# Seven half-size products for each matrix product of an MLP, with operands of the second stage stored by the first

## The chip, the cores and the metric

The kernel runs on one core of a Trainium2 chip. The core has five engines that run side by side, each through its own instructions in order: TensorE (PE in the profile; PEld is its weight load), VectorE (DVE), ScalarE (ACT), GpSimd (POOL) and SyncE (SP), which here only issues DMA transfers. Matmuls read SBUF and add into one of eight PSUM banks (512 float32 a partition each); DVE and ACT read the banks, POOL can't. DMA engines carry data between DRAM and SBUF. The metric is the time of one execution on the device in microseconds; lower is better.

## What is computed

One layer of a decoder on 2048 tokens of width 1024, in float32: four kinds of token mixers, an output projection with gated residual, and an MLP with gated residual. Only the MLP's computation matters here:

```python
D_MODEL = 1024; SEQ = 2048; D_FF = 4 * D_MODEL
...
        y = jnp.concatenate([y_a, y_b, y_c, y_d], axis=-1) @ w_out[l]
        x = x + (gate1[:, None, :] * y).astype(x.dtype)

        h = _modulate(x, norm_ff_gain[l], shift2, scale2)
        y = jnp.square(jax.nn.relu(h @ w_ff1[l])) @ w_ff2[l]
        x = x + (gate2[:, None, :] * y).astype(x.dtype)
```

`h` is 2048 x 1024, `w_ff1` 1024 x 4096, `w_ff2` 4096 x 1024. To keep float32 accuracy every product in the kernel is three matmuls: an operand is split into a high part that PE takes as it is (float32r) and the low remainder, and high x high, high x low and low x high are added in the bank.

## The kernel before

The program is written with a library that places semaphores by itself and orders the instructions of each engine by a plan of its own; priorities are the order of the program, with exceptions marked `high_priority`. All transfers named below are issued by SP, in order.

*Mixing stage* (up to about 1895 us). Two strands are woven: `strand_a` is attention over four chunks of 512 tokens, `strand_b` the projections, the two recurrent mixers and, per chunk, `w_out_dense` (output projection, L1279) and `second_norm` (L1313). `second_norm` makes the MLP's input: four PE transposes to a bank, ACT scales and shifts it, DVE casts the high part and POOL subtracts to get the low part (`modulate`, L551 to L558); both are stored in DRAM as `h2h_d` and `h2l_d`, one 256 KB piece for each chunk and each k-tile of 128 channels.

*Memory.* Two arenas, `AR` (float32r) and `AF_` (float32), are cut into slots by hand: in `AR` the normalised input `hTh`, `hTl` (32 KB a partition), `LS` and `QS` (attention's keys, values and queries), `TS`, `KS` (high and low parts on their way out); in `AF_` `FA` (attention's rows), `FB` (everything else) and `raws` (weights as loaded). `whi` and `wlo` are two buffers each for the split weights. `w_out_dense` takes its input in the `hTh`/`hTl` space or, after attention, in the `LS`/`QS` space (`hts`, L1331).

*MLP* (from about 1895 us). The tokens go in two halves of 1024 (`hf`). For each half, 16 blocks `b` of 256 hidden columns: `load_w` brings and splits 1 MB of `w_ff1` (ACT casts, POOL subtracts, `split_w` L188), `load_w2` 1 MB of `w_ff2`. For each of two chunks `cc`, `ff1` (L1470) runs 2 x 8 k-tiles x 3 matmuls into one of three banks; ACT applies Relu and Square, DVE squares, POOL subtracts, so that the hidden activations stay in SBUF as high and low parts `rh`, `rl`. `ff2` (L1487) of the chunk before then runs 4 token blocks x 2 column halves x 6 matmuls into one of five banks, and DVE adds each bank to the accumulator `acc` in SBUF (L1508). In the last two blocks of a half the gate is applied, the residual added and the output stored (L1511 to L1516). Each matmul loads 128 x 128 weights and streams 512 columns.

## Time and profile before

| | |
|---|---|
| Median of 3 runs | 3331.63 us (3330.45 to 3335.48) |
| The profiled execution | 3335.55 us, span of its instructions 3333.7 us |
| PE busy, share of the span | 94% |
| DVE, ACT, POOL busy | 55%, 42%, 41% |
| Matmuls | 18166, of which 6144 in the six lines of the MLP |
| Transfers | 427.01 MB, mean 128 GB/s |
| Mean granted TensorE clock | 0.954 of full speed |

The page gives the busy time of each engine over the whole span and in 40 slices; a share over the span mixes the two stages, so the stretches are asked for one by one. A busy PE includes the overlap of one matmul with the next: the number of matmuls in a stretch tells more than their durations. "Granted clock" is the clock that TensorE was allowed, 1.00 being 2.4 GHz and 0.50 being 1.2 GHz.

### The profile page before, as it was taken

To read this page: it belongs to the slowest core of one execution; us is meant where nothing else is said; L and a number is where in the kernel's file an instruction comes from. 1 tells how busy PE (TensorE), PEld (TensorE's weight loads), DVE (VectorE), ACT (ScalarE), POOL (GpSimd) and SP (SyncE) were. 2 spreads that over 40 slices of the span, in tenths; PEclk is the share of its full clock that TensorE was granted. 3 is DMA by queue.
4 is the path that set the end of the run, shared out by engine and by line. 5 is a ranking of instruction groups with operands and counts; after the bars stand their busy time and mean duration, and the time that the engine had idled before them with its cause. 6 is when DMAs were issued, how large, how long until landed. Compare 5 with 4: busy or idle time off the path is not lost.

```text
span 3333.7 us, 50269 instructions
## 1 busy us (share of the span) xinstructions
PE 3130.8 (94%) x18166; PEld 2621.7 (79%) x18166; DVE 1842.0 (55%) x4146; ACT 1391.6 (42%) x3004; POOL 1370.4 (41%) x1136
## 2 busy tenths in 40 slices
PE   6999999898888999998897899999999999999999
PEld 4898989687676888887685888888888888888887
DVE  4466577877779686767877323333235423333336
ACT  3666666455455566655555332222211221221111
POOL 4454343243243455454441533333335533333327
PEclk8999999799897999999897899999999999999999
DMA  7876667345334554463435621111113411111112
GB/s 252 268 270 212 220 228 228 121 124 176 98 119 150 169 159 128 155 224 88 129 105 173 229 79 51 51 51 51 39 46 125 171 51 51 51 50 40 43 46 101
DMA packets 342620, 427.01 MB, mean 128 GB/s; under 512 B 33161, under 2 KB 229860, under 8 KB 340308
## 3 DMA queue, kind: packets, MB, share of 16 engines
q1 hardware_dynamic: 337764, 415.42, 38.8%
q10 hardware_dynamic: 4608, 8.39, 0.7%
q8 instruction: 143, 2.34, 0.3%
q14 instruction: 105, 0.86, 0.1%
HBM read 318.72 MB, written 104.99 MB: 127 GB/s over the span
## 4 chain that ended last, share of the span: by engine, by line
PE 46%; DVE 2%; ACT 1%; DMA 1%; issue 0%; POOL 0%; POOLq 0%; SPq 0%; DVEq 0%; ACTq 0%
PE bank L1504 7%; PE bank L1503 7%; PE bank L1502 7%; PE bank L1478 7%; PE bank L1477 7%; PE bank L1479 7%; PE bank L513 1%; DVE AF L873 1%; PE bank L514 1%; PE bank L515 1%; DVE AF L678 0%; ACT AF L687 0%; PE bank L671 0%; PE bank L138 0%; PE bank L740 0%
## 5 line engine op out<-in xcount | busy, mean ns | idle before, releaser
L193 POOL TENSOR_TENSOR wlo<-AF,whi 128x512 fp32r<-128x512 f32 (+2 forms) x432 | 716.0, 1674 | 612.1 <-ACT whi L190 556.3
L1508 DVE TENSOR_TENSOR AF<-bank,AF 128x512 f32<-128x512 f32 x448 | 306.3, 689 | 470.3 <-PE bank L1504 467.6
L513 PE MATMUL bank<-whi,AR 128*128 128x256 f32 (+1 forms) x1664 | 491.2, 296 | 22.0 <-DMA AR<-yh 11.0
L190 ACT ACTIVATE whi<-AF 128x512 fp32r<-128x512 f32 (+2 forms) x432 | 318.3, 756 | 456.4 <-PE bank L1504 256.9
L515 PE MATMUL bank<-whi,AR 128*128 128x256 f32 (+1 forms) x1664 | 481.5, 291 | 1.5 <-DMA AR<-yl 1.5
L514 PE MATMUL bank<-wlo,AR 128*128 128x256 f32 (+1 forms) x1664 | 482.4, 290 | 0.0
L1484 POOL TENSOR_TENSOR AR<-AF,AR 128x512 fp32r<-128x512 f32 x128 | 166.4, 1300 | 615.5 <-DVE AF L1483 482.8
L1478 PE MATMUL bank<-AR,whi 128*128 128x512 f32 x1024 | 404.8, 395 | 0.0
L1477 PE MATMUL bank<-AR,whi 128*128 128x512 f32 x1024 | 402.1, 393 | 1.6 <-DMA AR<-h2h 1.6
L1503 PE MATMUL bank<-wlo,AR 128*128 128x512 f32 x1024 | 403.6, 394 | 0.0
L1504 PE MATMUL bank<-whi,AR 128*128 128x512 f32 x1024 | 403.6, 395 | 0.0
L1502 PE MATMUL bank<-whi,AR 128*128 128x512 f32 x1024 | 403.5, 394 | 0.0
L1479 PE MATMUL bank<-AR,wlo 128*128 128x512 f32 x1024 | 402.5, 393 | 0.0
L687 ACT ACTIVATE AF<-AF,att_m 128x512 f32<-128x512 f32 (+3 forms) x480 | 311.9, 652 | 163.1 <-DVE att_m L684 153.9
L1481 ACT ACTIVATE AF<-bank 128x512 f32<-128x512 f32 x128 | 76.0, 595 | 706.0 <-PE bank L1479 691.6
L513 PEld LDWEIGHTS bank<-whi,AR 128*128 128x128 f32 x1664 | 325.3, 196 | 34.4 <-DMA AR<-yh 12.5
L1483 DVE TENSOR_TENSOR AF<-AF 128x512 f32<-128x512 f32 x128 | 125.6, 982 | 410.1 <-ACT AR L1482 410.1
L515 PEld LDWEIGHTS bank<-whi,AR 128*128 128x128 f32 x1664 | 323.7, 195 | 6.4 <-issue 2.5
L514 PEld LDWEIGHTS bank<-wlo,AR 128*128 128x128 f32 x1664 | 325.4, 196 | 2.8 <-issue 1.0
L678 DVE TENSOR_SCALAR_CACHE_REDUCE AF<-bank 128x512 f32<-128x512 f32 (+3 forms) x480 | 284.9, 604 | 69.8 <-PE bank L671 37.8
L671 PE MATMUL bank<-AR 97*128 97x512 f32 (+10 forms) x640 | 240.5, 431 | 63.4 <-DVE AF L678 60.7
L740 PE MATMUL bank<-AR 128*128 128x256 f32 (+1 forms) x1152 | 234.5, 310 | 11.7 <-DVE AR L730 9.3
(305 smaller groups left out, 5780.1 us busy)
## 6 DMA issues: line engine op xcount, KB each, us to landing
AF<-in_w_ff SPq DMA_DIRECT2D x128, 512.0 KB
AF<-in_w_in SPq DMA_DIRECT2D x144, 256.0 KB
AF<-in_w_in SPq DMA_DIRECT2D x192, 128.0 KB
AF<-in_w_ada SPq DMA_DIRECT2D x80, 256.0 KB
AR<-kD SPq DMA_DIRECT2D x80, 224.0 KB
AF<-in_x SPq DMA_DIRECT2D x64, 256.0 KB
AF<-in_w_out SPq DMA_DIRECT2D x64, 256.0 KB
AR<-kA SPq DMA_DIRECT2D x40, 256.0 KB
```

The source lines that it names most:

```text
L190: nc.scalar.activation(h, r, AF.Copy)
L193: nc.gpsimd.tensor_tensor(l, r, f32(h), ALU.subtract)
L513: nc.tensor.matmul(o[:, :n], hTh[:, k, t], h[:, k, :n], start=(k == 0), stop=False)
L514: nc.tensor.matmul(o[:, :n], hTh[:, k, t], l[:, k, :n], start=False, stop=False)
L515: nc.tensor.matmul(o[:, :n], hTl[:, k, t], h[:, k, :n], start=False, stop=(k == KT - 1))
L687: nc.scalar.activation(FA[e][:, :w], FA[e][:, :w], AF.Exp, scale=-1.0, bias=mx, accum_out=sz[:, p:p + 1] if n > 1 else z)
L1477: nc.tensor.matmul(o, W[0][:, k, js], h2h[k][:, ct], start=(k == 0), stop=False)
L1478: nc.tensor.matmul(o, W[0][:, k, js], h2l[k][:, ct], start=False, stop=False)
L1479: nc.tensor.matmul(o, W[1][:, k, js], h2h[k][:, ct], start=False, stop=(k == KT - 1))
L1502: nc.tensor.matmul(o, rh[:, j, ts_], W[0][:, j, us], start=(j == 0), stop=False)
L1503: nc.tensor.matmul(o, rh[:, j, ts_], W[1][:, j, us], start=False, stop=False)
L1504: nc.tensor.matmul(o, rl[:, j, ts_], W[0][:, j, us], start=False, stop=(j == 1))
```

## The change

Each product of the MLP, `h @ w_ff1` and `relu(...)**2 @ w_ff2`, is computed by Winograd's form of Strassen's method, one level deep. The operands are seen as 2 x 2 blocks; seven products of blocks, of sums of blocks on both sides, give the four blocks of the result.

*First stage.* For each half of the tokens (`ps_`), `h_operands` loads the four pieces of a k-tile in float32 and makes seven operands, each split by ACT and DVE (`split2`). For each of 16 groups of 256 hidden columns, `Weights.ahead` loads 1 MB of `w_ff1` and makes seven weight operands, up to ten ahead. Products run in the order 1, 5, 6, 2, 7, 3, 4, each 4 k-tiles x 3 matmuls. In the middle groups 1, 6, 7 and 4 add into one bank and 5 and 3 into another, 2 has its own; `up_evict` copies or adds out of the bank between products. In the first and last group of each half the k-tile is the outer loop, over seven banks (`up_evict7`). `up_whole` applies Relu and Square on ACT, makes the seven operands of the second stage by sums on DVE and stores them as `r_d`, in runs of 128 float32.

*Second stage.* The products run one after the other over all eight pairs of token blocks, each with its own bank, in the order 1, 6, 7, 4, 5, 3, 2; the contraction is 16 k-tiles in two halves `h`. `w_operand` loads blocks of `w_ff2` and sums and splits them, `r_operand` loads and splits the activations. Banks are copied by ACT after products 1, 6 and 7 while they go on adding, and `dn_out` finishes an output block after 4, 5, 3 and 2.

*Around it.* `second_norm` stores one float32 piece instead of two parts and is finished inside the mixing stage instead of beside the first MLP blocks. The arenas are cut into tiles of their own in a pool `mix`, in the order FA, TS, KS, AL (LS and QS), AH (hTh and hTl), ST, FB, raws; the pools of the MLP are laid over them, tile by tile, and a new tile waits for the old tiles under it. The tiles of the second stage lie over those of the first in the same way. The MLP has no POOL instruction.

The core of the diff:

```diff
@@ second_norm
-                hi, lo = ring(KS), ring(KS)
-                modulate(o, hi, lo, A2[:, k:k + 1], mod[:, SH2 + k:SH2 + k + 1])
-                nc.sync.dma_start(h2h_d[c][k], f32(hi))
-                nc.sync.dma_start(h2l_d[c][k], f32(lo))
+                f = FB.get()
+                nc.scalar.activation(FB[f][:, :512], o, AF.Identity, scale=A2[:, k:k + 1],
+                                     bias=mod[:, SH2 + k:SH2 + k + 1])
+                nc.sync.dma_start(h2_d[c][k], FB[f][:, :512])
+                FB.put(f)
@@ strand_b
-            left.append((rest, st["h"][0] is hTh))
+            for _ in rest:
+                yield
...
+    mix_pool.__exit__(None, None, None)
+    UO = (1, 5, 6, 2, 7, 3, 4)
+    both = ctx.enter_context(tc.tile_pool(name="mlp", bufs=1, reuse_waits="tile"))
+    NTMP, NWA = 12, 2
+    temps = Slots([both.tile([P, 512], F32, name=f"tmp{i}") for i in range(NTMP)])
+    stage = Slots([both.tile([P, 2048], F32, name=f"stage{i}") for i in range(2)])
+    wu = [tuple(t.rearrange("p k n -> p (k n)")[:, u * 512:(u + 1) * 512] for t in w.tiles)
+          for w in (whi, wlo) for u in range(4)]
+    def split2(dst, x):
+        hi, lo = dst
+        nc.scalar.activation(hi, x, AF.Copy)
+        V(lo, x, f32(hi), ALU.subtract)
...
+    for kt in range(4):
+        for i in UO:
+            hc[i, kt] = tuple(up.tile([P, CT], F32R, name=f"hc{i}_{kt}{q}") for q in "hl")
+        if kt == 0:
+            wa = [tuple(up.tile([P, 512], F32R, name=f"wa{i}{q}") for q in "hl") for i in range(NWA)]
+    WS = Slots(wa + wu)
+    def h_operands(ps_, kt):
+        si = stage.get()
+        raw = stage[si].rearrange("p (q t) -> p q t", q=4)
+        for q in range(4):
+            nc.sync.dma_start(raw[:, q], h2_d[2 * ps_ + q % 2][kt + 4 * (q // 2)])
+        b11, b12, b21, b22 = (raw[:, q] for q in range(4))
+        split2(hc[1, kt], b11)
+        i1, t1 = combine(b12, b11, SUB)
+        split2(hc[5, kt], t1)
...
+        stage.put(si)
...
+    def up_mm(o, w, i, kt, first, last):
+        h, l = (t[:, kt * P:(kt + 1) * P] for t in WS[w])
+        xh, xl = hc[i, kt]
+        nc.tensor.matmul(o, h, xh, start=first, stop=False, skip_group_check=True)
+        nc.tensor.matmul(o, h, xl, start=False, stop=False, skip_group_check=True)
+        nc.tensor.matmul(o, l, xh, start=False, stop=last, skip_group_check=True)
...
+    def up_store(t, ps_, g, i):
+        nc.sync.dma_start(r_d[ps_][i][:, :, g, :], temps[t].rearrange("p (b t) -> p b t", t=P))
+    def up_evict(o, st, ps_, g, i):
+        if i == 1:
+            st["11"] = saved(o)
+        elif i == 5:
+            st["22"] = saved(o)
+        elif i == 6:
+            st["21"] = saved(o)
+        elif i == 4:
+            st["12"] = temps.get()
+            up_whole(st, ps_, g, i, o)
+        else:
+            k = {2: "11", 7: "22", 3: "21"}[i]
+            V(temps[st[k]], o, temps[st[k]], ADD)
+            up_whole(st, ps_, g, i)
...
+    wts.ahead()
+    for kt in range(4):
+        h_operands(0, kt)
+    for ps_ in range(2):
+        for g in range(NG):
+            st = {}
+            if g in (0, NG - 1):
+                os_ = {i: ring(allb) for i in UO}
+                for kt in range(4):
+                    for i in UO:
+                        wts.ahead()
+                        up_mm(os_[i], wts.slot[ps_, g, i], i, kt, kt == 0, kt == 3)
+                        if kt == 3:
+                            WS.put(wts.slot[ps_, g, i])
+                            up_evict7(os_, st, ps_, g, i)
+                    if g and not ps_:
+                        h_operands(1, kt)
+            else:
+                oa, oc = ring(allb), ring(allb)
+                for i in UO:
+                    wts.ahead()
+                    o = oa if i in (1, 6, 7, 4) else oc if i in (5, 3) else ring(allb)
+                    for kt in range(4):
+                        up_mm(o, wts.slot[ps_, g, i], i, kt, kt == 0 and i in (1, 5, 2), kt == 3 and i in (4, 3, 2))
+                    WS.put(wts.slot[ps_, g, i])
+                    up_evict(o, st, ps_, g, i)
+    up_pool.__exit__(None, None, None)
...
+    def r_operand(i, p_, kq):
+        w = rd[i, p_, kq] = RS.get()
+        r = raw2.get()
+        nc.sync.dma_start(raw2[r].rearrange("p (k n) -> p k n", n=P), r_d[p_ // TB][i][:, p_ % TB, 4 * kq:4 * kq + 4, :])
+        split2(RS[w], raw2[r])
+        raw2.put(r)
...
+    for i in DO:
+        for h in range(2):
+            for p_ in range(8):
+                o = banks[p_]
+                ahead(1)
+                for u in range(2):
+                    rs = rd[i, p_, 2 * h + u]
+                    rh, rl = RS[rs]
+                    for k in range(4):
+                        kk = KH * h + 4 * u + k
+                        wh, wl = DS[wd[i, kk]]
+                        c = slice(k * P, (k + 1) * P)
+                        nc.tensor.matmul(o, rh[:, c], wh, start=(i in (1, 5, 2) and kk == 0), stop=False, skip_group_check=True)
+                        nc.tensor.matmul(o, rh[:, c], wl, start=False, stop=False, skip_group_check=True)
+                        nc.tensor.matmul(o, rl[:, c], wh, start=False, stop=(kk == NK - 1 and i in (4, 3, 2)), skip_group_check=True)
+                        if p_ == 7:
+                            DS.put(wd[i, kk])
+                    RS.put(rs)
+                    ahead(0)
+                if h == 0:
+                    continue
+                if i in C:
+                    nc.scalar.activation(C[i][p_], o, AF.Copy)
+                else:
+                    dn_out(o, p_, i)
```

## Rows read from the trace of the kernel before

**Rows 1.** The page: the span, and the busy time of PE.

```profile
span 3333.7 us, 50269 instructions
...
PE 3130.8 (94%) x18166; PEld 2621.7 (79%) x18166; DVE 1842.0 (55%) x4146; ACT 1391.6 (42%) x3004; POOL 1370.4 (41%) x1136
```

**Rows 2.** Stretches: length, busy us of PE, PEld, DVE, ACT, POOL; clock, DMA, GB/s.

```profile
1895.00:3329.00 1434.00, 1431.75 (x6193) 1160.54 (x6192) 523.75 (x686) 309.36 (x428) 552.50 (x310) 1.00 0.21 68
...
2000.00:2200.00 200.00, 200.00 (x864) 162.17 (x863) 66.49 (x90) 42.34 (x56) 71.16 (x38) 1.00 0.17 53
...
2600.00:2620.00 20.00, 20.00 (x88) 16.23 (x87) 13.47 (x17) 2.47 (x4) 10.24 (x8) 1.00 0.64 248
```

**Rows 3.** Grouped instructions, 2000 to 3000 us: busy, mean ns | idle before them.

```profile
L1478 PE MATMUL bank<-AR,whi 128*128 128x512 f32 x720 | 284.5, 395 | 0.0
...
L1504 PE MATMUL bank<-whi,AR 128*128 128x512 f32 x717 | 282.9, 395 | 0.0
```

**Rows 4.** Matmuls of one line: ns min/median/max, first and last start.

```profile
L1477 PE MATMUL bank<-AR,whi x1024: 387/393/501, 1895.0 to 3305.3; 128*128 128x512 f32 x171
...
L1504 PE MATMUL bank<-whi,AR x1024: 388/393/476, 1919.6 to 3328.0; 128*128 128x512 f32 x171
```

**Rows 5.** Elementwise work by line, same columns.

```profile
L1508 DVE TENSOR_TENSOR AF<-bank,AF x448: 674/692/693, 1971.2 to 3297.5; 128x512 f32<-128x512 f32 x150
...
L1483 DVE TENSOR_TENSOR AF<-AF x128: 678/693/2512, 1910.7 to 3307.5; 128x512 f32<-128x512 f32 x128
...
L1481 ACT ACTIVATE AF<-bank x128: 577/599/602, 1909.1 to 3306.2; 128x512 f32<-128x512 f32 x128
...
L1482 ACT ACTIVATE AR<-AF x128: 623/634/644, 1910.0 to 3306.8; 128x512 fp32r<-128x512 f32 x128
...
L1484 POOL TENSOR_TENSOR AR<-AF,AR x128: 1284/1293/1738, 1911.5 to 3308.9; 128x512 fp32r<-128x512 f32 x128
```

**Rows 6.** Instructions in order of time at 2104 us: start, duration.

```profile
2104.39 2.41 POOL L193 TENSOR_TENSOR wlo<-AF,whi 128x1024 fp32r<-128x1024 f32 x1 [0.37 <-ACT whi L190]
...
2105.49 1.85 DVE L1483 TENSOR_TENSOR AF<-AF 128x512 f32<-128x512 f32 x1
```

**Rows 7.** First and last start, by line: projection, MLP loads, attention's output.

```profile
L515 PE MATMUL bank<-whi,AR x1664: 274/281/1202, 45.0 to 1894.8; 128*128 128x256 f32 x170, 128*128 128x268 f32 x15
...
L1523 SPq DMA_DIRECT2D AR<-h2h x32: 319/376/668, 1758.1 to 2598.2; - x32
...
L489 DVE TENSOR_TENSOR AR<-AF,AR x24: 668/693/1762, 203.7 to 1835.7; 128x512 fp32r<-128x512 f32 x24
```

**Rows 8.** Chain of waits about the MLP's start: start, duration, what.

```profile
1790.72 2.56 DMA AR<-yh
...
1895.34 5.66 DMA AR<-h2l
1901.01 6.13 DMA AR<-h2h
```

**Rows 9.** Stretches about the MLP's start, columns as in rows 2.

```profile
1840.00:1850.00 10.00, 5.97 (x27) 5.38 (x27) 3.15 (x13) 4.32 (x14) 0.00 (x0) 0.50 0.52 178
1850.00:1860.00 10.00, 10.00 (x81) 9.77 (x81) 5.77 (x11) 5.15 (x8) 6.87 (x7) 0.94 0.36 135
1860.00:1870.00 10.00, 10.00 (x88) 10.00 (x87) 4.77 (x6) 2.74 (x5) 9.29 (x9) 1.00 0.73 250
...
1880.00:1890.00 10.00, 10.00 (x87) 10.00 (x86) 1.70 (x4) 3.86 (x8) 9.08 (x9) 1.00 0.45 148
...
1900.00:1910.00 10.00, 8.34 (x41) 6.10 (x41) 6.02 (x18) 2.80 (x6) 2.06 (x2) 1.00 1.00 355
```

**Rows 10.** DMA in 1400:1500, 2010:2400, 2590:2620: packets, MB, share of 16 engines.

```profile
q1 hardware_dynamic: 20912, 22.19, 68.4%
...
q1 hardware_dynamic: 11556, 18.30, 15.2%
...
DMA packets 4813, 8.45 MB, mean 282 GB/s; under 512 B 448, under 2 KB 1460, under 8 KB 4811
```

More of the change, by code (lines that the diff above doesn't have):

```diff
@@ L1361, in hybrid_block @@
         ada_blocks = iter(range(8, 24))
-        left = []
         def strand_b():
@@ new lines, in hybrid_block, with saved @@
+    wts = Weights()
+    def up_mm(o, w, i, kt, first, last):
[4 more added lines that the diff above has]
+        nc.tensor.matmul(o, l, xh, start=False, stop=last, skip_group_check=True)
+    def saved(o):
+        t = temps.get()
+        nc.scalar.activation(temps[t], o, AF.Copy)
+        return t
```

332 lines of the change are left out of this document (214 added, 118 removed).

## The prediction

> **What bounds the kernel now.** I read the busy table of the page first, then the tenths over the span, then cuts of the span into stretches. The page has TensorE (PE) at 94% of 3333.7 us [rows 1], but that is a mean of two different stages. From the first MLP matmul to the last there are 1434 us, PE is busy for 1431.75 of them, and the granted clock is 1.00 (2.4 GHz) throughout; VectorE (DVE) is busy for 37%, ScalarE (ACT) for 22% and GpSimd (POOL) for 39% [rows 2]. In the grouped instructions of the middle 1000 us the idle column of the matmul lines is 0.0 [rows 3]. So in the MLP nothing but PE sets the time, and a matmul taken away is worth its spacing there. That is not the 395 ns of the duration column, which overlaps with the next one: 864 matmuls start in 200 us [rows 2], 0.2315 us each. The spacing doesn't move where transfers are dense: 88 in 20 us at a DMA share of 0.64 [rows 2].
>
> **What is taken away.** Six matmul lines (the first and the last in [rows 4]) of 1024 each are 6144. After the change the first stage has 2 halves x 16 groups x 7 products x 4 k-tiles x 3 passes = 2688 and the second 7 x 8 x 16 x 3 = 2688, all of the same shape (128 columns of weights, 512 streamed). That is 5376, 768 fewer, and 768 x 0.2315 = 177.8 us. The sum starts at the profiled execution's 3335.55 us and ends at it less 177.8 if PE streams as before; the rest is what keeps it from streaming.
>
> **What is added on DVE and ACT.** A middle group of the first stage (12 of its matmuls per product, 84 in all) lasts 84 x 0.2315 = 19.4 us on PE. DVE has in it 7 subtractions for the low parts of the weights, 4 sums of weight quarters, 3 additions out of a bank and 4 sums for the second stage's operands, 18. One costs 0.69 us, from a bank or from SBUF [rows 5]: 12.5 us. ACT has 7 high parts, 3 copies and 8 Relu/Square, 18 at 0.60 to 0.63 us [rows 5], 11.2 us. Both lie beside PE. I take the median; the longest DVE square took 2.51, and the one of 1.85 us that I looked at lay under a POOL subtraction of 2.41 us [rows 6]. No POOL instruction is left in the new MLP. Even at 1.0 us each the 18 would stay under the 19.4. In the second stage a step of one bank (24 matmuls) is 5.6 us; DVE has 2 low parts of activations, 1 to 3 operations for a weight and up to 3 for the output, at most 6 x 0.69 = 4.2 us.
>
> **Hand-overs of a bank.** A middle group keeps one bank for products 1, 6, 7, 4 and one for 5, 3. PE must wait until ACT has copied product 1 before 6, product 6 before 7, and until DVE has added product 7 before 4. Behind the waiting matmul stands all of PE's queue. The cover is one product, 12 x 0.2315 = 2.8 us, and the copy or addition needs 0.6 to 0.7. It runs out when three other operations stand ahead on that engine. I take 0.2 us a group, 28 groups, **+6 us**; bounds 0 and 2 us a group (56 us), the upper one being three operations ahead twice in a group.
>
> **Start of the first stage.** Here the change loses most. Now the first MLP matmul starts at 1895.0, 0.2 us after the last one of the output projection [rows 4, 7], because half of its operands were loaded from 1758 on, as ready high and low parts [rows 7]. After the change the operands must be made. Their memory is that of the mixing stage, laid over it in order: the scratch and staging tiles over FA, free when attention ends at about 1836 [rows 7], but the k-tile-0 operands and two weight buffers mostly over KS and AL. AL holds the last projection's input (its other half, AH, was free at 1758, so the loads went there [rows 7]) until 1894.8, and the eight weight buffers cut from whi and wlo are free only then too. From 1895: seven weight operands (DVE 4.9 us, some sums earlier), which release the only staging tile that `h_operands` can have, +6; then four rounds of a 256 KB load, 2.6 us [rows 8], and 11 DVE operations, 7.6 us, one after the other since they share that tile, 4 x 11 = +44; then the last matmuls, +1. That is 51 us for a group with 19.4 us of PE work, and an estimated 5 us for the 49 matmuls beside the MLP's 6144 [rows 2], so **+26 us**. Bounds: +14 if the loads hide behind DVE (55 operations x 0.69 = 38), +40 if a load takes the 5.7 to 6.1 us that the present ones take at the same place [rows 8] and the last norm's own DVE work falls in between. I take the shorter load, since what runs beside it then is one load and not sixteen.
>
> On the clock: from 1840 to 1850, with PE idle for 4 of 10 us, its granted clock was 0.50 (1.2 GHz), and 0.94 in the next 10 us at full work [rows 9]; a dip of PE to 8.3 of 10 us at 1900 left it at 1.00 [rows 9]. The Trainium skill ("TensorE: Matmul & The Clock Gate", section "HAM oscillation — how this bites in real kernels") says that a kernel which waits for operands between its k-tiles falls back to half clock at each of them. The traces so far bear both out.
>
> **Between the halves.** The last group of the first half and the first of the second run k-tile outermost on seven banks. The operands of k-tile 0 may be overwritten 21 matmuls = 4.9 us into the last group; four rounds of 10.5 us end at 47, with the 11 evictions of that group (7.6 us of DVE) partly between them, at most 54. PE wants k-tile 3 at 19.4 + 14.6 = 34. So 13 to 20, **+16 us**; the lower bound is 2, if loads hide (44 x 0.69 + 4.9 = 35).
>
> **From first to second stage.** The weights' buffers lie over k-tile 0 and are made under the last 14.6 us of PE. The activations' buffers come free one by one in the last round and need ACT and DVE, 1.3 us, but the 7.6 us of evictions are in the same DVE queue. Bounds 1.3 and 10, **+6 us**.
>
> **Ahead of the MLP.** The second norm drops 32 casts on DVE and 32 subtractions on POOL (1.3 us each in the MLP [rows 5]) and half of its stores, all beside other work; the mixing stage's tiles are cut anew, which lets the planner order the work differently. I count 0, with bounds of -10 and +15. The last matmul starts at 3328.0 and the span ends at 3333.7 [rows 1, 4], 5.7 us later; the new end is one bank's three DVE operations and a store, the same. The 2 us that PE idles in the MLP now [rows 2] go.
>
> **Sum.** 3335.55 - 177.8 + 6 + 26 + 16 + 6 - 2 = 3209.8 for an execution like the profiled one. The median of the runs shown, 3331.63, lies 3.9 lower: **3206 us**.
>
> **DMA.** Each group of the first stage stores 7 x 256 KB in runs of 512 B and loads 1 MB in runs of 1 KB: 7 x 512 + 1024 = 4608 packets in 19.4 us. Packets averaging 1.06 KB took 68.4% x 16 x 100 us / 20912 = 52 ns in one stretch; in the MLP, averaging 1.6 KB, 15.2% x 16 x 390 us / 11556 = 82 ns [rows 10]. At 52 ns a group's transfers need 4608 x 52 / 16 = 15.0 us, so they hide; most of the new packets are smaller than either mean, so 52 is the nearer row. In the second stage a step moves at most 1.5 MB in 5.6 us, 270 GB/s; 8.45 MB went in 30 us (282 GB/s) at the busiest stretch of the MLP without PE losing a matmul [rows 2, 10]. The Trainium skill ("DMA: Bandwidth & Descriptors", section "Specifications") puts the smallest transfer for line rate at 512 B, just the size of these runs; no store of that size was singled out here.
>
> **The rivals.**
> 1. *Bank hand-overs stall every middle group.* For: DVE and ACT run 12.5 and 11.2 of 19.4 us in strict order, and three different chains share them. Against: the cover is four times one operation. At the 2 us bound, 28 x 2 = 56 instead of 6: 3256. Chance 0.17.
> 2. *The stores bind the first stage*, the case on the other side. If a packet costs the 82 ns of the MLP's own stretch, a group needs 4608 x 82 / 16 = 23.6 us, 4.2 more than PE, x 32 = 134, nearly all of the gain left: 3206 + 134 = 3340. It decides from 81 ns on (a loss of 126 us). For: the number is a row; small runs, written to memory, have no row of their own. Against: bytes, not packets, seem to carry the cost, since the stretch with the larger packets has the higher price. Chance 0.08.
> 3. *The transitions hide.* If the planner makes operands early and loads run ahead, the terms of 26, 16 and 6 shrink to their lower bounds, 14, 2 and 1: 3175. For: DVE is busy for 4.8 of the 10 us from 1860 and 1.7 of those from 1880 [rows 9]. Against: the memory is not free. Chance 0.10.
> 4. *The clock falls between the k-tiles*, at the start and between the halves. A round's 21 matmuls then take 9.7 instead of 4.9 us, still under the 10.5 of DVE and load, except in the last round of each: +5, and +5 while the second group speeds up: 3216. Chance 0.12. It is the Trainium skill's rule named above that would bring this about.
> 5. *The new cut of the tiles lengthens the mixing stage* by 15 us or more, or its end frees memory later: 3225 to 3240. Chance 0.07.
> That the work isn't reduced is excluded by the loops counted above.
>
> **How the numbers follow.** Forecast 0.46, rivals 0.17, 0.08, 0.10, 0.12, 0.07. The range is 3160 (all lower bounds, -10 ahead of the MLP) to 3280: it leaves out rival 2, the worst third of rival 1 and little below. A measurement of this kernel tells 0.2% (7 us) from no change. Faster 0.92, within 0.2% 0.02, slower 0.06; the last two are rival 2.
>
> **What would show it.** Right: 5376 matmuls of 512 in the MLP, 0.23 us apart within groups; PE idle at three places, with DVE or a load named as releaser; POOL at zero there; DVE at 0.69 us. Wrong: PE waits spread evenly over the groups, put down to ACT copies or DVE additions (rival 1), or a DMA share near 0.9 in the first stage with stores behind (rival 2); a first MLP matmul well before or after 1900 to 1910; a spacing other than 0.2315.

## The result and the profile after

The changed kernel takes 3226.77 us (median; its runs go from 3212.16 to 3231.48), the kernel before, measured beside it, 3333.35: a ratio of 0.967, 95% interval 0.964 to 0.971. That is 106.6 us less where 126 were forecast, inside the range of 3160 to 3280. The profiled execution took 3222.74 us, its span 3221.0.

The page of the changed kernel, busy us of the span (before: [rows 1]):

```profile
span 3221.0 us, 50522 instructions
...
PE 2973.0 (92%) x17398; PEld 2494.0 (77%) x17398; DVE 2053.9 (64%) x4642; ACT 1650.5 (51%) x3576; POOL 777.6 (24%) x800
```

Stretches of it, columns as in [rows 2]: a stretch of middle groups of the first stage, the change from the first stage to the second, and the only part of the second stage where PE waits:

```profile
2000.00:2240.00 240.00, 240.00 (x1043) 196.66 (x1042) 152.66 (x238) 135.30 (x231) 0.00 (x0) 1.00 0.52 154
...
2560.00:2620.00 60.00, 52.04 (x207) 41.70 (x206) 33.20 (x58) 26.21 (x47) 0.00 (x0) 0.89 0.69 221
...
2900.00:3000.00 100.00, 94.91 (x398) 73.66 (x397) 52.63 (x84) 28.83 (x52) 0.00 (x0) 1.00 0.68 217
```

In the middle groups PE is busy for all of the 240 us at a clock of 1.00, as before. VectorE is now at 0.64 there (0.33 in the 200 us of [rows 2]), GpSimd has nothing left, and the DMA share is 0.52. The MLP lasted 1433.2 us, from the last output-projection matmul (1894.8, [rows 7]) to the last matmul (3328.0, [rows 4]); now it lasts 1312.7, to 3215.6. The projection's last matmul itself comes 8.1 us later. One line of it, columns as in [rows 4]:

```profile
L523 PE MATMUL bank<-whi,AL x128: 275/280/582, 1837.9 to 1902.9; 128*128 128x256 f32 x128
```

From here on *lost* time is the length of a stretch less its MLP matmuls times their spacing, which is 0.2303 us within the first stage (19.35 us for a group of 84) and 0.2313 in the second. The places in order, for all kernels that ran; "later" is the rest of the second stage. Each row is one profiled execution, and a figure is good to some 0.3 us:

| kernel | last projection matmul | start | middle of a half | between halves | change of stage | later | span |
|---|---|---|---|---|---|---|---|
| changed kernel | 1902.9 | 36.7 | 0.0 | 9.7 | 16.1 | 9.5 | 3221.0 |
| e1_h2_pool | 1922.6 | 28.6 | 0.0 | 10.9 | 15.8 | 11.4 | 3235.5 |
| e1b_h2_last | 1909.5 | 28.5 | 0.0 | 11.7 | 15.7 | 13.0 | 3224.6 |
| e3_gate | 1907.0 | 35.9 | 0.3 | 9.7 | 17.7 | 10.2 | 3228.5 |
| e10_scratch | 1904.0 | 35.6 | 0.0 | 9.9 | 4.9 | 9.1 | 3211.5 |
| e4_dn_pool | 1904.6 | 36.0 | 0.0 | 10.1 | 15.8 | 11.1 | 3228.0 |
| e11_lag | 1900.8 | 35.7 | 0.0 | 9.7 | 15.8 | -0.4 | 3207.7 |
| e5_all | 1908.7 | 28.5 | 0.0 | 10.8 | 20.1 | 10.0 | 3233.1 |
| e12_rows | 1873.1 | 36.4 | 0.3 | 7.4 | 15.1 | 8.4 | 3187.1 |
| e13_all | 1866.5 | 27.4 | 0.3 | 6.7 | 5.0 | -0.5 | 3153.5 |
| e9_nosum | 1907.0 | 30.4 | 0.0 | 0.0 | 11.9 | 4.2 | 3199.7 |

The first row adds up: 5376 matmuls are 2688 x 0.2303 + 2688 x 0.2313 = 1240.8 us, and 72.0 lost make 1312.8. Where the gate's rows were moved, the last group of the first stage loses another 2 us, which no column shows.

### The profile page after: what moved, and what is told of

It reads as the page before. It is cut to its first block, busy times and chain, and to the rows that moved or that the text cites. A ratio compares the mean times of both kernels' runs of the same rounds, so it can differ in the third digit from the quotient of the medians.

```text
span 3221.0 us, 50522 instructions
## 1 busy us (share of the span) xinstructions
PE 2973.0 (92%) x17398; PEld 2494.0 (77%) x17398; DVE 2053.9 (64%) x4642; ACT 1650.5 (51%) x3576; POOL 777.6 (24%) x800
## 4 chain that ended last, share of the span: by engine, by line
PE 53%; DVE 13%; DMA 6%; ACT 3%; issue 2%; POOL 1%; SPq 0%; DVEq 0%; POOLq 0%; ACTq 0%
PE bank L1560 6%; PE bank L1561 6%; PE bank L1559 5%; PE bank L1782 5%; PE bank L1781 5%; PE bank L1780 5%; PE bank L142 3%; PE bank L521 2%; PE bank L748 2%; PE bank L523 2%; PE bank L522 2%; PE bank L679 2%; PE bank L734 2%; DMA stage<-in_w_ff 2%; DVE FA L881 2%
## 5 line engine op out<-in xcount | busy, mean ns | idle before, releaser
L197 POOL TENSOR_TENSOR wlo<-raw,whi 128x512 fp32r<-128x512 f32 (+1 forms) x304 | 408.7, 1364 | 387.1 <-ACT whi L194 346.0
L521 PE MATMUL bank<-whi,AH 128*128 128x256 f32 (+1 forms) x1536 | 452.3, 295 | 25.1 <-ACT whi L194 11.1
L522 PE MATMUL bank<-wlo,AH 128*128 128x256 f32 (+1 forms) x1536 | 445.7, 290 | 0.9 <-POOL wlo L197 0.9
L523 PE MATMUL bank<-whi,AH 128*128 128x256 f32 (+1 forms) x1536 | 444.8, 290 | 0.0
L695 ACT ACTIVATE FA<-FA,att_m 128x512 f32<-128x512 f32 (+3 forms) x480 | 310.5, 650 | 153.4 <-DVE att_m L692 146.2
L686 DVE TENSOR_SCALAR_CACHE_REDUCE FA<-bank 128x512 f32<-128x512 f32 (+3 forms) x480 | 284.3, 603 | 69.6 <-PE bank L679 40.0
L521 PEld LDWEIGHTS bank<-whi,AH 128*128 128x128 f32 x1536 | 299.1, 195 | 35.9 <-ACT whi L194 11.4
L522 PEld LDWEIGHTS bank<-wlo,AH 128*128 128x128 f32 x1536 | 299.4, 195 | 3.8 <-POOL wlo L197 1.4
L523 PEld LDWEIGHTS bank<-whi,AH 128*128 128x128 f32 x1536 | 298.4, 195 | 2.7 <-issue 1.9
L679 PE MATMUL bank<-AL 97*128 97x512 f32 (+10 forms) x640 | 241.9, 436 | 57.1 <-DVE FA L686 53.8
L748 PE MATMUL bank<-TS,AL 128*128 128x256 f32 (+1 forms) x1152 | 238.4, 314 | 15.7 <-DVE TS L738 7.2
L734 PEld LDWEIGHTS bank<-ident,FA 128*128 128x128 f32 x1088 | 139.7, 150 | 38.5 <-DVE FA L881 28.5
L509 PE MATMUL bank<-AH,whi 128*128 128x512 f32 x384 | 159.1, 419 | 7.1 <-DVE FB L1107 2.1
L510 PE MATMUL bank<-AH,whi 128*128 128x512 f32 x384 | 159.0, 414 | 2.5 <-DMA AH<-hl 2.5
```

Source lines behind the costliest of these rows:

```text
L197: nc.gpsimd.tensor_tensor(l, r, f32(h), ALU.subtract)
L521: nc.tensor.matmul(o[:, :n], hTh[:, k, t], h[:, k, :n], start=(k == 0), stop=False)
L522: nc.tensor.matmul(o[:, :n], hTh[:, k, t], l[:, k, :n], start=False, stop=False)
L523: nc.tensor.matmul(o[:, :n], hTl[:, k, t], h[:, k, :n], start=False, stop=(k == KT - 1))
L679: nc.tensor.matmul(o[:, :w], lh, rh(p)[:, :w], start=(i == 0), stop=(i == len(mm) - 1 and not diag))
L686: nc.vector.tensor_scalar(FA[e][:, :w], o[:, :w], -1.0, 3.0e38, ALU.mult, ALU.min, accum_out=st[:, p:p + 1])
```

## The experiments

All are edits of the changed kernel, except b_rows, which edits the kernel before. Moving an issue to another queue moves the waits that it stands in, and leaves the bytes and the arithmetic as they were.

### The start of the first stage: e1_h2_pool, e1b_h2_last, e9_nosum

The chain of waits in the changed kernel (start, duration, what), and SyncE's issues in order of time:

```profile
1917.00 6.78 DMA stage<-in_w_ff
1923.80 1.29 DVE tmp L1472 x2
```

```profile
1910.97 0.99 SPq L1330 DMA_DIRECT2D h<-FB  x2
...
1912.98 3.97 SPq L1330 DMA_DIRECT2D h<-FB  x5
1917.00 1.20 SPq L1529 DMA_DIRECT2D stage<-in_w_ff  x2
```

The first load of w_ff1 (L1529) is issued 14.1 us after the last projection matmul, straight behind the last second-norm store (L1330), and lands 6.78 us later. VectorE has nothing from 1910 until that load has landed at 1923.8; then it is the bound:

```profile
1920.00:1930.00 10.00, 0.31 (x1) 0.31 (x2) 6.20 (x11) 4.74 (x9) 0.00 (x0) 0.50 0.68 233
1930.00:1940.00 10.00, 8.84 (x26) 6.17 (x25) 10.00 (x17) 5.73 (x11) 0.00 (x0) 0.66 0.39 127
1940.00:1950.00 10.00, 9.18 (x35) 5.88 (x34) 10.00 (x18) 6.32 (x12) 0.00 (x0) 1.00 0.55 172
1950.00:1960.00 10.00, 9.02 (x37) 6.47 (x36) 10.00 (x18) 5.35 (x10) 0.00 (x0) 1.00 0.20 64
```

```diff
-                nc.sync.dma_start(h2_d[c][k], FB[f][:, :512])
+                nc.gpsimd.dma_start(h2_d[c][k], FB[f][:, :512])        # e1_h2_pool
+                (nc.gpsimd if c == NC - 1 else nc.sync).dma_start(...)  # e1b_h2_last
```

> The stores of the second normalisation's result are issued by GpSimd and no longer by SyncE; nothing else changes. Theory, the queue: in the changed kernel the first load of first-layer weights was issued at 1917.0, on SyncE right behind the last of these stores, 14 us after the last output-projection matmul (1902.9). With the stores on another queue SyncE reaches that load once the output projection's own transfers are issued, at about 1905, so the load lands about 12 us earlier, VectorE begins on the operands at about 1912 in place of 1923.8, and the first MLP matmul comes 9 to 12 us after the last output-projection matmul or a little more (26.8 us before): a gain of 8 to 11 us up to the first steady group. Rival, VectorE sets the start: it has the second normalisation until about 1910 and then the sums of the weights, so an earlier load gains 0 to 2 us.

Measured: the start loses 28.6 us in place of 36.7, the gain of 8 that the queue predicted. The span is longer all the same, since the mixing ended at 1922.6; more on that below. e5_all has the same stores on GpSimd and its mixing ended at 1908.7, so what the move costs ahead of the MLP can't be read from one execution. The next kernel leaves the other chunks alone:

> Only the last chunk's stores of the second normalisation are issued by GpSimd; the other chunks' stay on SyncE. Theory, SyncE's queue: the start of the first stage loses about 8 us less than the 36 us of the changed kernel, as when all chunks' stores were moved (28.5 us in both executions), and the mixing ends as in the changed kernel, 1903 to 1907, so that the gain is seen in the span: 8 us. Rival, the loss at the start follows the end of the mixing and not the queue: 34 us or more.

Measured: 28.5. The load now follows the projection by 2 us:

```profile
1911.47 1.19 SPq L1529 DMA_DIRECT2D stage<-in_w_ff  x2
```

The queue is shown as the cause of 8 us. The span was 3224.6, no better than the changed kernel's: its mixing ended 6.6 us later with PE's order unchanged, and 2.0 and 3.5 us more were lost between the halves and late in the second stage, so the gain is read at the place and not in the total.

```diff
-        i1, t1 = combine(b12, b11, SUB)
-        split2(hc[5, kt], t1)
-        i2, t2 = combine(b22, t1, SUB)
-        split2(hc[6, kt], t2)
+        split2(hc[5, kt], b12)
+        split2(hc[6, kt], b22)
...
```

> The changed kernel without the four sums that make the activations' operands (7 in place of 11 VectorE operations a k-tile): the operands that need a sum take a quarter as it is, so the result is another one; transfers, matmuls and splits are as they were. Theory, VectorE sets the start once the loads are there (10.00 of 10 us busy from 1930 to 1950): four k-tiles of four sums at 0.60 us are 9.6 us, and the loss between the last output-projection matmul and 2000 falls from 36 to 27 us, that between the halves (9.7 us) by 2 to 6. Rival, the staging tile and its loads set it: within 3 us of 36.

Measured: 30.4 at the start, a gain of 6.3, and 9.7 to 0.0 between the halves, more than the 2 to 6 expected. VectorE was still busy for 28.52 us of 1930 to 1960, but PE streamed through the halves' change:

```profile
2250.00:2270.00 20.00, 20.00 (x88) 16.38 (x87) 19.06 (x33) 14.47 (x28) 0.00 (x0) 1.00 0.77 237
2270.00:2290.00 20.00, 20.00 (x88) 16.42 (x87) 19.09 (x32) 15.08 (x28) 0.00 (x0) 1.00 0.66 203
```

So VectorE's operations on operands set the pace of the ramp after the first load, and without the four sums the halves' change costs nothing. In the changed kernel VectorE isn't the last link there, though: 5.9 of the 9.7 us are lost where PE waits for splits of weights behind a weight load that left late (see "Between the halves" below). That the change of stage and the second stage, whose code is the same, lost less as well (11.9 and 4.2) was not expected; the order on the queues differs from there on, and I have no run that tells why.

### The change of stage: e3_gate, e10_scratch

The chain of waits in the changed kernel:

```profile
2574.60 5.11 DMA tmp<-r
...
2579.78 5.99 DMA r<-tmp
...
2585.87 0.30 DVE tmp L1742
...
2586.30 2.05 PE bank L1743 x8
```

An operand load (r), the last operand store, VectorE's gate rows (L1742) in a scratch tile that this store gives back, and the gate's small matmuls, behind which the products stand. Moving them ahead of the last group:

```diff
             st = {}
+            if ps_ and g == NG - 1:
+                gt = [gate_bank(u) for u in range(2)]   # in a ring bank and two of the later scratch tiles
...
-    gate2 = [gate_bank(u) for u in range(2)]
+    gate2 = [temps[t] for t in gt]
```

> The two rows of the second gate are spread over the partitions ahead of the last group of the first stage, and no longer at the start of the second. Theory, the gate's place in the queues: TensorE lost 15.5 us between the stages (2569 to 2600), since the gate's eight small matmuls stand in its queue among the first products and wait for scratch that the last operand store gives back (5.4 us twice). Moved ahead, the loss between the stages falls to about 8 us, which is the fall of operand store, load and first product, and the last group of the first stage loses at most 2 us more: gain 6 to 8 us. Rival, the operands' way through memory sets it: the first product of the second stage waits for the stored operands whatever the gate does, and the loss stays within 2 us of 15.5.

Measured: 17.7 us. The gate's place was not what set it. PE's longest wait there, and the chain:

```profile
PE bank L1783 <- ACT wlo L1465: 10.6, 1, 10.6
```

```profile
2580.56 5.18 DMA r<-tmp
...
2585.76 4.85 DMA tmp<-in_w_ff
...
2590.63 0.64 ACT wd3h L1465
```

ScalarE stood at the split of a weight (wd3h) whose load (tmp<-in_w_ff) had to wait for the same last store (r<-tmp) to leave its scratch tile; the split of the operand that PE wanted was behind it in ScalarE's queue. So the next kernel keeps the five scratch tiles out of the ring at first:

```diff
+    held = [raw2.free_.pop() for _ in range(5)]
...
+                if i == DO[0] and h == 0 and p_ == 3:
+                    raw2.put(*held)
                 ahead(1)
```

> The second gate's rows are made ahead of the last group of the first stage, as in the run that moved them alone, and the first weight and operand loads of the second stage use only the eight quarters of the staging tiles; the five scratch tiles of the first stage join them from the fourth group of products on. Theory, the scratch tiles: a weight load that reuses one waits until the last group's result has been stored from it (the store was issued at 2580.6 and took 5.2 us, the load 4.9 us), and ScalarE, which works in order, holds the operands' split behind that weight's: TensorE waited 10.6 us at 2582.6. With the scratch tiles held back the loss between the stages (17.7 us with the gate moved, 16.1 us in the changed kernel) falls to 8 us or less. Rival, the transfers at the change (0.65 to 0.7 of the DMA engines busy there) set it: 12 us or more, since fewer tiles mean fewer loads under way.

Measured: 4.9 us, and fewer tiles under way did no harm (the DMA share even rose, to 0.77):

```profile
2560.00:2620.00 60.00, 57.57 (x240) 46.07 (x239) 36.14 (x57) 27.79 (x49) 0.00 (x0) 0.97 0.77 261
```

Either cure alone leaves the other wait on the same store; I ran the gate's alone, not the scratch tiles' alone.

### The second stage: e4_dn_pool, e11_lag

```diff
-        nc.sync.dma_start(temps[ti], x1_d[t][:, us])
+        nc.gpsimd.dma_start(temps[ti], x1_d[t][:, us])
...
-        nc.sync.dma_start(out[0, t * P:(t + 1) * P, us], x)
+        nc.gpsimd.dma_start(out[0, t * P:(t + 1) * P, us], x)
```

> In the second stage the loads of the residual and the stores of the result are issued by GpSimd and no longer by SyncE. Theory, the order on SyncE: the loads of second-layer weights stand there behind a residual load that waits for a scratch tile whose store was issued just ahead of it, so the weights of the next product came late, and TensorE lost 8.5 us at 2930 to 3000 and 1.4 us at about 2705. With the two kinds of transfer on another queue that loss is gone: gain 7 to 10 us. Rival, the load's own traffic or VectorE's sums set it: the loss stays at 7 us or more. The start of the MLP and the change of stage are the changed kernel's own here, so that they also show how far these vary from one execution to the next.

Measured: 9.4 us lost at 2900 to 3010 where the changed kernel loses 8.5: the order on SyncE was not the cause, my theory fell. And the end came later: 9.5 us from the last matmul to the end of the span in place of 5.4, with the last store on GpSimd. What VectorE waited for in the changed kernel at 2900 to 3000 (us in total, times, longest):

```profile
DVE stage L1702 <- DMA stage<-in_w_ff: 24.5, 9, 3.6
DVE tmp L1702 <- DMA tmp<-in_w_ff: 11.7, 4, 3.6
```

13 waits, 36 us: before each subtraction for a weight of the fifth product VectorE stands for a load just issued, and the low part of an operand that PE needs now is queued behind. The cure is to issue the load a step earlier:

```diff
-                w_operand(*wtodo.pop(0))
+                if not loaded:
+                    loaded.append(w_load(*wtodo.pop(0)))
+                if wtodo[1:]:
+                    loaded.append(w_load(*wtodo.pop(0)))
+                w_operand(*loaded.pop(0))
```

> In the second stage the loads of each weight operand are issued one step (5.5 us) ahead of the subtraction and split that read them. Theory, order on VectorE and ScalarE: in the fourth product's second half the fifth product's weights are loaded, two blocks each, and VectorE stands up to 4.2 us before each subtraction (14 waits, 40 us in 2900 to 3000) with the split of an operand that TensorE needs now behind it: TensorE loses 0.5 to 1.3 us a group, 8.5 us in all. With the loads a step earlier the loss of 2900 to 3010 falls to 2 us or less, and that at about 2718 (1.1 us) too. Rival, the 13 scratch tiles and the transfers (0.68 busy, 217 GB/s) set the pace, so an earlier load only waits longer for its tile: 6 us or more.

Measured: nothing is lost any more, though more bytes move in that stretch (238 GB/s, 217 before the edit):

```profile
2900.00:3000.00 100.00, 100.00 (x435) 81.91 (x433) 60.50 (x95) 33.95 (x60) 0.00 (x0) 1.00 0.76 238
```

The span of 3207.7 is 13.3 below the changed kernel's: 9.9 of it here, 2.1 from a mixing that ended earlier.

### The first three moves together: e5_all

> The three moves together: the second normalisation's stores and the second stage's residual loads and result stores go by GpSimd, and the gate's rows are made ahead of the last group of the first stage. Theory, order on the queues is what the changed kernel loses: the gains add up to 21 to 29 us, so 3194 to 3206 us where the changed kernel has a median of 3226.8 and a profiled run of 3222.7. Rival, the three places are limited by transfers and VectorE: 3219 to 3227 us.

Measured: 3234.28 us (3233.07 to 3238.02), slower than the changed kernel. The start's 8 us were gained, the change of stage lost 4 more, the tail was 12.4 us in place of 5.4, and the mixing ended 5.8 later. The tail, the change of stage and the 2 us in the last group of the first stage, some 13 us, are the price of having taken two causes from the names of the waits alone; why the mixing ended later isn't shown.

### Ahead of the MLP: e12_rows, b_rows

Matching VectorE instructions run 16 to 21 us later than in the kernel before from 190 to 1500 us. Some 12 us of it are there by 120 us. Stretches of the kernel before, then of the changed one:

```profile
60.00:80.00 20.00, 19.85 (x155) 19.63 (x154) 5.48 (x14) 6.74 (x17) 7.14 (x8) 0.94 0.74 254
80.00:100.00 20.00, 19.39 (x146) 18.55 (x147) 8.91 (x20) 11.21 (x25) 13.00 (x11) 1.00 0.97 316
```

```profile
60.00:80.00 20.00, 11.01 (x87) 10.03 (x85) 3.03 (x9) 3.88 (x11) 2.48 (x5) 0.83 0.48 159
80.00:100.00 20.00, 14.62 (x96) 14.09 (x97) 3.14 (x12) 7.71 (x15) 10.30 (x9) 0.75 0.91 301
```

PE's weight port waits there for the input projection's weights, once and long:

```profile
PEld bank L521 <- ACT whi L194: 11.4, 1, 11.4
```

SyncE's loads of w_in stop after six and go on 41 us later, behind 48 small stores of constant rows (L454 to L471), 24 of them from the lines that the diff touched (L468, L471):

```profile
36.02 2.95 SPq L208 DMA_DIRECT2D raw<-in_w_in  x6
...
71.16 0.58 SPq L468 DMA_DIRECT2D qB<-FA  x1
71.78 1.15 SPq L471 DMA_DIRECT2D qD<-FA  x2
...
80.25 2.96 SPq L208 DMA_DIRECT2D raw<-in_w_in  x6
```

In the kernel before twelve loads had gone ahead of its rows, from 36.3 to 41.8.

```diff
-                nc.sync.dma_start(qB_d[c][u][P:P + 4, :]...
+                nc.gpsimd.dma_start(qB_d[c][u][P:P + 4, :]...
...
-                    nc.sync.dma_start(qD_d[c][u][384 + 2 * h:386 + 2 * h, :]...
+                    nc.gpsimd.dma_start(qD_d[c][u][384 + 2 * h:386 + 2 * h, :]...
```

> The constant rows of the attention operands (24 small stores, 0.58 us of SyncE each) are issued by GpSimd in place of SyncE. Theory, the recut's rows: in the changed kernel TensorE has no product from 69.1 to 84.5, since the loads of the input projection's weights stop at 38.5 on SyncE and go on at 80.3, behind these rows, where in the kernel before six more loads had gone ahead of them (to 41.8); matching VectorE instructions ran 16 to 21 us later than before from about 190 to 1500, of which 8 us were left at the end of the mixing. With the rows on another queue the hole of 15 us goes, and the last output-projection matmul comes 8 to 17 us earlier than the changed kernel's own (1902.9 to 1907 in three executions): 1888 to 1897, total 3210 to 3219. Rival, the attention's own chain sets the end of the mixing: the hole goes, but the 15 us are waited for later and the end stays within 4 us of 1905.

Measured: 3189.87 us (3184.58 to 3203.52), 0.957 of the kernel before, interval 0.954 to 0.960, and 36.9 below the changed kernel. Twelve loads go ahead again, and PE is busy in the hole:

```profile
37.00 7.02 SPq L208 DMA_DIRECT2D raw<-in_w_in  x12
```

```profile
60.00:80.00 20.00, 15.96 (x130) 15.52 (x129) 3.68 (x14) 6.56 (x17) 17.61 (x22) 1.00 0.75 255
80.00:100.00 20.00, 20.00 (x154) 19.87 (x155) 8.13 (x18) 8.43 (x20) 8.08 (x8) 0.91 0.98 313
```

```profile
L523 PE MATMUL bank<-whi,AL x128: 275/280/583, 1808.6 to 1873.1; 128*128 128x256 f32 x128
```

The projection ended 29.8 us earlier, more than the 8 to 17 expected, and 21.7 before the kernel before's own: against that kernel matching VectorE instructions were 6 us late at 200, even at 1130, 6 early at 1500 and 20 early at 1600. So the hole is shown, and its undoing is worth the larger part of the 15 us by 200 (10 us) and all of it by 600; what else made the rest is open. Is it the rows in themselves? The kernel before with its rows moved:

```diff
-                nc.sync.dma_start(qB_d[c][u][P:P + 4, :]..., negr)
+                nc.gpsimd.dma_start(qB_d[c][u][P:P + 4, :]..., negr)
-                nc.sync.dma_start(qD_d[c][u][384:388, :]...
+                nc.gpsimd.dma_start(qD_d[c][u][384:388, :]...
```

> The kernel before, with nothing changed but that its 16 constant-row stores (8 for each of two operands) are issued by GpSimd. It tells what of the 30 us that the move gave the changed kernel's mixing is the undoing of a loss and what is a gain of its own. Theory, the changed kernel's hole alone: the kernel before has no such hole (its six further weight loads go ahead of the rows), so it stays within 4 us of its 3336 us, and the recut tiles themselves make the mixing some 20 us shorter (last output-projection matmul at 1873.1 with them, 1894.8 before). Rival, the rows stand in the way in both: the kernel before gains 10 to 22 us too, and its last output-projection matmul comes at 1873 to 1885.

Measured: neither. 3360.99 us, 1.008 of the kernel before (1.006 to 1.010), the projection's end at 1919.6, and a hole of its own: no product of the projection starts from 47.0 to 63.5, and PE is idle from 47.2 to 57.2. VectorE and GpSimd there, in order of time:

```profile
45.66 9.35 DVE L344 COPY AF<-AF 32x128 f32<-32x128 f32 x2
48.28 6.73 DVE L374 TENSOR_TENSOR AF<-AF 1x64 f32<-1x64 f32 x1
```

```profile
42.40 4.37 POOL L462 DMA_DIRECT2D qB<-AF  x8 [1.20 <-DVE AF L456]
46.79 1.33 POOL L193 TENSOR_TENSOR wlo<-AF,whi 128x536 fp32r<-128x536 f32 x1
...
52.30 2.57 POOL L193 TENSOR_TENSOR wlo<-AF,whi 128x536 fp32r<-128x536 f32 x2
```

GpSimd issued the rows from 42.4 to 46.8, and the work it had put off ran without a break to 54.9. Until then VectorE stood in the second of two small copies and in a 1x64 product, 9.27 us and 6.73 (they overlap and end together at 55.0; the first copy took 0.20); in the kernel before the two copies took 1.55 and the product 1.32. PE's next matmul needed what VectorE makes behind them. Matching VectorE instructions were 14 us later than in the kernel before at 210 and 25 only from 1800 on, so the hole is at most some 14 of the 25; the rest is open. So the move of the rows is worth what the order around it makes of it, +25 us in one kernel and -30 in the other, and it doesn't isolate what the new cut of the tiles does by itself.

### How far the other engines are: e7_twopass

```diff
     nc.tensor.matmul(o, h, xh, start=first, stop=False, skip_group_check=True)
-    nc.tensor.matmul(o, h, xl, start=False, stop=False, skip_group_check=True)
     nc.tensor.matmul(o, l, xh, start=False, stop=last, skip_group_check=True)
```

> The first stage without the product of the weights' high part with the activations' low part: 1792 matmuls in place of 2688 there, 56 in place of 84 a group, so the result is less exact; all other work is left. It shows how far the other engines are from setting the pace. A group takes 19.35 us now, with VectorE busy 0.64 of it (12.3 us), ScalarE 0.56 (10.9 us) and 154 GB/s. Theory, bank hand-overs and VectorE are hidden also at this pace: a group takes 56 x 0.2303 = 12.9 us and the first stage 206 us less, about 433 us in place of 638.6. Rival, hand-overs or VectorE come next at once: 14 us or more a group, 465 us or more, and the clock may fall in the waits.

Measured: the middle groups of the first half take 12.95 to 13.3 us, those of the second half mostly 14.0 to 14.4 (a few 13 to 15.6), and the first stage 486.3 us. In the first half the hand-overs are hidden even at two thirds of the time, to 0.1 us a group in the mean; in the second ScalarE waits for scratch tiles that are being stored (r<-tmp, 18.4 us in 2250 to 2405). Two of its stretches:

```profile
1960.00:2130.00 170.00, 165.08 (x701) 133.21 (x702) 148.00 (x239) 128.90 (x238) 0.00 (x0) 0.99 0.76 220
2250.00:2400.00 150.00, 141.45 (x592) 110.82 (x591) 117.71 (x187) 102.08 (x188) 0.00 (x0) 1.00 0.71 207
```

The total is above both figures (433 and 465): the first three groups cost 12 us more over their pace than in the changed kernel, the halves' change 23, and the second half's groups some 16.

### The four that helped: e13_all

The edits of e1b_h2_last, e10_scratch, e11_lag and e12_rows in one kernel.

> The four moves that helped, together: the constant rows by GpSimd, the last chunk's second-normalisation stores by GpSimd, the gate's rows ahead of the last group with the scratch tiles held back, and the second stage's weight loads one step ahead. Theory, four places with nothing in common: the gains add up, 8 + 12 + 9 us on the 3189.9 us of the kernel with the rows moved: 3156 to 3168 us. Rival, part of each is waited for again elsewhere (the start of the first stage waits for VectorE, the halves' change for loads): 3170 to 3185 us.

Measured: 3158.31 us (3155.22 to 3160.55), 0.9465 of the kernel before, interval 0.945 to 0.948, 68.5 us below the changed kernel. The gains add up: 27.4 at the start, 5.0 at the change of stage, nothing later. The mixing, too, ended 6.6 us earlier than in e12_rows, with the same order of PE's work, so part of the total is spread.

## Why the prediction was right, and where it was not

The total is right because the main step is, and because errors of 6 to 10 us at seven places partly cancel, which is luck. Against the sum for the profiled execution (3209.8; measured 3222.7), term by term in us:

| step | foreseen | measured | difference |
|---|---|---|---|
| 5376 matmuls streamed | 1248.4 (1433.2 - 177.8, less 2 and 5 named in the text) | 1240.8 | -7.6 |
| hand-overs | 6 | 0.0 | -6 |
| start, with 5 us of other matmuls | 31 | 36.7 | +5.7 |
| between the halves | 16 | 9.7 | -6.3 |
| change of stage | 6 | 16.1 | +10.1 |
| second stage | 0 | 9.5 | +9.5 |
| ahead of the MLP | 0 | 8.1 | +8.1 |

They add to 13.5, against the 12.9 that are missing.

**Matmuls taken away.** Right, and PE streams in both stages. The spacing of 0.2315 was read low: the 864 matmuls of the 200 us count those that reach over the stretch's edges. By the sum's own 1433.2 us less 7, one of the 6144 matmuls took 0.2321 us before. It is now 0.2303 and 0.2313, which over 5376 matmuls makes about 7 of the -7.6; why it fell isn't shown.

**Hand-overs, rival 1.** The cover of one product was the right argument, the 0.2 us a group an allowance for nothing. VectorE's 0.69 us for an operation held (whi<-stage: median 684 ns over 111), and from the fourth group of a half on none lost time. Ahead of that PE did wait for a bank's copy (L1559 behind ACT L1565), in the third group of the first half and the second of the second, 1.3 us in two waits. e7_twopass shows that the cover holds at 12.95 us a group.

**Start.** The size is nearly right by luck, the reason is not. I had the first weights made from 1895 on and a load in series with VectorE in each round (2.6 + 7.6 = 10.2 us, which I took as 11: 3 us too much in four rounds). But the mixing's pool ends as one, and every MLP instruction stands behind every mixing instruction on its queue: the first load left at 1917.0 behind the last second-norm store. So the first MLP matmul came at 1929.7, well after the 1900 to 1910 that the prediction had named, and by its own sign this part of it was wrong. What saved the size is that, once the first load had landed, loads hid behind VectorE (10.00 of 10 us), whose operations started 0.60 us apart and not 0.69, so the ramp was shorter than four rounds. "Each queue that it is moved past" was the question I didn't put to SyncE. e1b_h2_last and e9_nosum show both parts.

**Between the halves.** Too dear by 6.3, and neither the value's rounds nor the lower bound's "loads hide" is what happened. The first group of the second half lost 3.2 us. The group behind it, which the prediction left out, lost 5.9: PE waited there for splits of weights on ScalarE (wlo, L1465), and ScalarE for a weight load that left SyncE only at 2274.51 and took 8.0 us. Ahead of that load stood VectorE's last sum of operands (done at 2273.3) and, on the same queue, stores; which of the two held it isn't shown. The load, and PE's matmuls behind it:

```profile
2274.51 8.00 DMA stage<-in_w_ff
...
2284.78 0.70 PE bank L1559
2285.49 0.43 PE bank L1560
...
2289.17 0.23 PE bank L1561
```

Without the four sums the same load left at 2263.39, and nothing was lost (e9_nosum).

**Change of stage.** I had looked at the buffers of the activations and at VectorE's queue. What set it is a third resource, the scratch tiles from which the last operands are still being stored: weight loads and gate rows wait for them, and ScalarE's order passes the wait on. The upper bound of 10 was too low by 6.

**Second stage.** "No loss" was wrong. I had counted VectorE's time in a step (at most 4.2 of 5.6 us) and not that it works in order: an instruction that waits for a load holds those behind it however idle the engine is (0.53 busy).

**Ahead of the MLP, rival 5.** The bounds of -10 and +15 held, the value of 0 did not. The mechanism is rival 5's only in name: with the same tiles twelve loads of w_in go ahead once the rows are moved (e12_rows), so it was the order on SyncE, in which the planner put six of them behind the rows. Why it did is open.

**DMA, rival 2.** It fell. In the first stage's second half (packets, MB, share of 16 engines):

```profile
q1 hardware_dynamic: 29656, 17.92, 60.0%
```

0.600 x 16 x 100 / 29656 us = 32 ns a packet at a mean of 0.6 KB, less than the 52 and far from the 81 from which it would have decided. The Trainium skill ("DMA: Bandwidth & Descriptors", section "Specifications") wants transfers of 512 B for line rate; with runs of just that size the trace agrees so far that their price went down with their bytes.

**The clock, rival 4.** In part. The granted clock was 0.50 at 1920 to 1930, with one MLP matmul there, then 0.66, and 1.00 from 1940 though PE idled for a tenth. Between the halves it dipped once:

```profile
2260.00:2270.00 10.00, 8.34 (x33) 5.92 (x33) 10.00 (x18) 4.90 (x10) 0.00 (x0) 1.00 0.34 107
...
2280.00:2290.00 10.00, 7.25 (x24) 5.19 (x23) 7.46 (x13) 5.15 (x10) 0.00 (x0) 0.83 0.39 116
```

At the change of stage it was 0.66, 0.76 and 0.89 from 2570 to 2600. The Trainium skill ("TensorE: Matmul & The Clock Gate", section "HAM oscillation — how this bites in real kernels") has the clock fall at each k-tile of a kernel that waits for operands there. Here it stayed at 1.00 through the four k-tiles of the second half's first group (2249 to 2272), though PE waited for operands in them. It fell once in the group behind, after the waits for weights, in the stretch in which PE was busy for 7.25 of 10 us. So the rival's rule didn't hold here, and the rows before had shown one fall and no series of them. What the clock cost can be estimated from the trace: at 0.50 matmuls start 0.43 us apart (2285.49, above), at 1.00 0.23 (2289.17). There are 9 so far apart at the start, 7 between the halves and 21 at the change of stage, so at most 1.8, 1.4 and 4.2 us, where the rival had +5 and +5; part of it PE would have spent waiting.

**The spread.** The four runs of the changed kernel spread over 19 us, those of the kernel before over 5 beside them and over 13 in all comparisons (3327.6 to 3340.4). Part of it is ahead of the MLP: eight executions with the same order of PE's work there ended the projection between 1895.4 and 1909.5, and mostly the later, the lower the mean granted clock of their first 1900 us: 0.922 (1895.4, e7_twopass), 0.918 (1902.9, the changed kernel), 0.914 (1904.6, e4_dn_pool), 0.912 (1909.5, e1b_h2_last). Which of the two brings the other isn't shown. The changed kernel and e4_dn_pool part at one place, by 6.5 us, of which 1.3 are left by 1130:

```profile
300.00:350.00 50.00, 45.28 (x316) 39.52 (x317) 36.48 (x94) 29.64 (x69) 21.58 (x21) 0.95 0.60 211
```

```profile
300.00:350.00 50.00, 45.82 (x258) 36.98 (x258) 36.00 (x92) 28.52 (x67) 18.71 (x17) 0.76 0.52 182
```

Why the clock fell in one execution and not in the other is open.

## What to carry to other kernels

Where one engine sets the pace, taking its instructions away pays in full in the steady part; forecast the seams by listing, for each queue in order, what stands ahead of the first instruction that the next stage needs, and which tile it waits for to come free. An engine's idle share is no cover for an instruction that stands behind a waiting one: issue loads a step ahead of their readers, and keep tiles whose stores are still under way out of the next stage's first loads. The name of a wait is a place to begin: here two of three cures read straight from the names were worth nothing, while the largest gain lay 1800 us ahead of the edit's own stage, in the order of some small stores.

## What the runs showed of the hardware

- While GpSimd ran without a break, a 1x64 product on VectorE took 6.73 us (1.32 in the kernel before) and a 32x128 copy 9.27, where the same copy had taken 0.20 just ahead (b_rows). The Trainium skill ("SBUF — State Buffer", section "Terms") says that the two engines share a port pair, that it is held for a whole instruction and that the loser stops altogether; the trace agrees that VectorE stops, for a 1x64 product of two SBUF tiles, and here one wait spans several GpSimd instructions. No run isolates the port as the cause.
- With the last store issued by GpSimd the span ended 9.5 and 12.4 us after the last matmul (e4_dn_pool, e5_all), with SyncE 5.4 (changed kernel).
- Packets of 0.6 KB on average took 32 ns each, those of [rows 10] 52 and 82: the price followed the bytes.
- A 128x512 matmul of the same form starts every 0.2303 us in one stage and every 0.2313 in the other, at a clock of 1.00 in both, and every 0.43 at 0.50.
